# Feed-forward input products of two token blocks formed as seven block products on sums of parts, with features kept in memory

## The chip, the cores and the metric

The kernel runs on 1 core of one Trainium2 chip. The metric is device time in microseconds (us) of one execution; the kernel before took 2666.41 us, the median of 3 runs (2663.89 to 2669.21).

## The reference

The reference is a two-layer encoder in fp32 on 1056 tokens (1024 of a prompt, 32 of a running stream) with 1024 features. Layer 0 mixes by a gated linear recurrence (HGRN2), layer 1 by sliding-window attention. Each mixer is followed by a SwiGLU feed-forward part with 2816 hidden features, and norms stand before and after each part:

```python
x = x + rms_norm(mix, norm_mix_post[layer])
hf = rms_norm(x, norm_ffn_pre[layer])
a, b = jnp.split(hf @ w_ffn_in[layer], 2, axis=-1)
x = x + rms_norm((jax.nn.silu(a) * b) @ w_ffn_out[layer], norm_ffn_post[layer])
```

The change concerns `hf @ w_ffn_in` above all, and the product with `w_ffn_out` behind it.

## The kernel before

**Layout.** Features lie on the 128 partitions, in 8 tiles (`KT`); tokens lie on the free axis in three blocks (`BL`): blocks 0 and 1 of 384 tokens, block 2 of 288. Every fp32 product is three passes of float32r matmuls on a high and a low part of both operands: high x high, high x low, low x high (`mm_fm`, L123 to L133, where L132 is the matmul). Products go to a pool of four PSUM buffers (`mmps`, tile `mm`).

**Weights.** `wunit` (L86 to L103) loads a unit of 128 x 1024 weights (512 KB) into one of two buffers `wst` by a DMA on SP (L90), casts it to `wh` on ACT (L101) and takes the low part `wl` on DVE (L102); `wh` and `wl` have four buffers each. Where a norm's weight is folded in, L97 and L98 do this in pieces.

**Norms.** `postnorm` (L208 to L253) finishes a block behind a mixer or a feed-forward part. It is a generator whose steps are called between other work (`go`, `step`). The sum of squares is taken on PE with a matmul by ones (L180), `newton` (L151 to L160) takes the inverse root on DVE in small operations, `rbcast` (L183 to L190) spreads it over the partitions: a diagonal `dm` on DVE (L185), a matmul by ones (L189) and a copy to `rb` on ACT (L190). Then the rows are scaled (L235), the old x is added (L236, loaded at L218), and `put_x` (L198 to L206) writes the next high and low parts `xh` and `xl`. The x is spilled to memory (L242). Behind a mixer, the scale of the next norm, `rb`, is not put into x: the feed-forward part starts on unscaled x, and `rb` is multiplied in when its products are evicted.

**The feed-forward part** (`ffn`, L256 to L377) has 22 hidden tiles j of 128. For each j and block b, `fin_half` (L264) forms the gate half and the up half, 24 matmuls each (8 feature tiles x 3 passes), from two units of `wfi`. `fin_ev` (L276 to L286) evicts: a multiply by `rb` (L281, L283, DVE), Silu (L282, ACT), a product (L284), and the hidden features' parts `gh` (L285, ACT) and `gl` (L286, DVE), which stay on the chip. `fout` (L320 to L344) forms the output products in parts of `FBLK` = 2, 4, 4, 4, 4, 4 hidden tiles; each part is added into `mix` on DVE (L337; the first copied on ACT, L335). The last part is done block by block, with its weights loaded again for each block, and the `postnorm` of the previous block runs beside it.

**Order.** Every engine takes its instructions in order. A scheduler places the instructions of DVE, ACT, SP and GpSimd (POOL) by priorities that follow the program's order; PE follows the program. The order of the work around the start of the feed-forward part is written by hand in `ffn` (calls of `fin_half` between `go(post1)` and `go(post)`, where `post1` is block 1's mixer norm and `post` block 2's), and in the tables that call steps of block 0's and 1's norms inside the mixers (`fill` in layer 0, `plan` in layer 1).

Of the kernel before, what the change touches and what calls it, by code (L numbers as in the profile page):

```python
# [27 lines left out]
FBLK = [2, 4, 4, 4, 4, 4]  # L28
# [30 lines left out]
def build(nc, tc, I, O):  # L59
# [26 lines left out]
    def wunit(src, scale=None, pieces=1):  # L86
# [16 lines left out]
        return wh, wl  # L103
# [104 lines left out]
    def postnorm(b, mix, acc, w2, xold, wnext, spill, yout, done, more=None):  # L208
# [20 lines left out]
        if yout is None:  # L229
            xs = newx(b)  # L230
            nacc = newacc(b)
        dst = spill if yout is None else yout
        for k in range(KT):
# [4 lines left out]
            if yout is None:  # L238
                put_x(b, k, m, xs, wnext)
                sq_acc(nacc, W, m, k == 0)  # L240
# [4 lines left out]
        if yout is None:  # L245
            done(xs, None, None)
# [9 lines left out]
    def ffn(L, nx, post1, post, wmix, w2, xold, wnext, spill, yout, res):  # L256
# [3 lines left out]
        gpc, gp = pool(f"fg{L}")  # L260
        gs = {}
        wu = {}

        def fin_half(j, b, half):  # L264
            if j not in wu:
                wu[j] = wpair(I[f"wfi{L}"], j)
            if j not in gs:
                gs[j] = (gp.tile([128, NT], F32R, tag="gh", name="gh", bufs=5),
                         gp.tile([128, NT], F32R, tag="gl", name="gl", bufs=5))
# [3 lines left out]
            mm_fm(ps, W, wu[j], 128 * half, lambda k: xh[:, k, :], lambda k: xl[:, k, :])  # L273
            return ps

        def fin_ev(j, b, pa, pb):  # L276
            c0, W = BL[b]
            rb = nx[b][2]
            gh, gl = gs[j]
            ta, tb = tmp(), tmp()  # L280
            nc.vector.tensor_tensor(ta[:, :W], pa[:, :W], rb[:, :W], mult)  # L281
            nc.scalar.activation(ta[:, :W], ta[:, :W], AF.Silu)  # L282
            nc.vector.tensor_tensor(tb[:, :W], pb[:, :W], rb[:, :W], mult)  # L283
            nc.vector.tensor_tensor(tb[:, :W], tb[:, :W], ta[:, :W], mult)  # L284
            nc.scalar.copy(gh[:, c0:c0 + W], tb[:, :W])  # L285
            nc.vector.tensor_tensor(gl[:, c0:c0 + W], tb[:, :W], gh[:, c0:c0 + W].bitcast(F32), sub)  # L286
# [3 lines left out]

        pa = fin_half(0, 0, 0)
# [12 lines left out]
        go(post)  # L304
# [6 lines left out]
        fin_ev(1, 2, pc, fin_half(1, 2, 1))  # L311
        for p in wmix:
            close(p)
        mpc, mp = pool(f"fm{L}", "right")
        mix = mp.tile([128, KT, NT], F32, tag="mix", name="mix")

        last = len(FBLK) - 1
        accs, ts = {}, {}

        def fout(fi, blocks):  # L320
            f = FBLK[fi]
            w = 1024 // f
            base = sum(FBLK[:fi])
            for u in range(f):
                unit = wunit(I[f"wfo{L}"][base + u])
                for m in range(w // 128):
                    k = u * (w // 128) + m
                    for b in blocks:
                        c0, W = BL[b]
                        ps = mmps()  # L330
                        mm_fm(ps, W, [unit], m * 128, lambda q: gs[base + q][0][:, c0:c0 + W],
                              lambda q: gs[base + q][1][:, c0:c0 + W], nk=f, width=w)
                        dst = mix[:, k, c0:c0 + W]
                        if fi == 0:
                            nc.scalar.copy(dst, ps[:, :W])  # L335
                        else:
                            nc.vector.tensor_tensor(dst, dst, ps[:, :W], add)  # L337
                        if fi == last:
                            if k == 0:
                                accs[b] = newacc(b)  # L340
                            sq_acc(accs[b], W, dst, k == 0)
                if fi == last and blocks[0] > 0:
                    for _ in range(steps[blocks[0]][4 + u]):
                        step(blocks[0] - 1)  # L344
# [13 lines left out]
        j = 2  # L358
        for fi in range(1, last):
            for q in range(FBLK[fi]):  # L360
                for b in range(NB):
                    fin(j, b)
                if q == 0:
                    fout(fi - 1, range(NB))
                j += 1


        steps = {1: (1, 2, 1, 1, 1, 0, 1, 1), 2: (1, 2, 1, 1, 1, 0, 0, 1)}
        for b in range(NB):
            for q in range(FBLK[last]):  # L370
                wu.pop(j + q, None)
                fin(j + q, b)
                if b == 0 and q == 0:
                    fout(last - 1, range(NB))
                if b > 0:
                    for _ in range(steps[b][q]):
                        step(b - 1)  # L377
            fout(last, [b])
# [44 lines left out]
    mbs = [mb, mb, None]  # L423
    os = [None] * NB
# [837 lines left out]
```

## Time and profile before

| | |
|---|---|
| median of 3 runs | 2666.41 us (2663.89 to 2669.21) |
| profiled execution | 2668.35 us, of which the span is 2666.6 us |
| granted TensorE clock, mean | 0.986 of full speed |
| DMA traffic | 237.28 MB, mean 89 GB/s |
| feed-forward part of layer 0 | about 670 to 1425 us of the span |
| feed-forward part of layer 1 | about 1870 us to the end |

In the profile, PE is TensorE's matmuls, PEld its weight loads, DVE VectorE, ACT ScalarE, POOL GpSimd and SP the engine that issues the DMAs. L132 is line 132 of the kernel. A group's row ends with the idle time of the engine just before its instructions and with what ended that wait. A waits row has the engine and line, what it waited for, and then total us, times and longest. The execution shown is one; the clock's column PEclk gives the share of full speed that was granted.

### The profile page before, as it was taken

To read this page: it belongs to the slowest core of one execution; us is meant where nothing else is said; L and a number is where in the kernel's file an instruction comes from. 1 tells how busy PE (TensorE), PEld (TensorE's weight loads), DVE (VectorE), ACT (ScalarE), POOL (GpSimd) and SP (SyncE) were. 2 spreads that over 40 slices of the span, in tenths; PEclk is the share of its full clock that TensorE was granted. 3 is DMA by queue.
4 is the path that set the end of the run, shared out by engine and by line. 5 is a ranking of instruction groups with operands and counts; after the bars stand their busy time and mean duration, and the time that the engine had idled before them with its cause. 6 is when DMAs were issued, how large, how long until landed. Compare 5 with 4: busy or idle time off the path is not lost.

```text
span 2666.6 us, 44419 instructions
## 1 busy us (share of the span) xinstructions
PE 2567.9 (96%) x17664; PEld 2466.6 (93%) x17664; DVE 1530.1 (57%) x3464; ACT 975.0 (37%) x2177; POOL 439.8 (16%) x652
## 2 busy tenths in 40 slices
PE   7999998998999999999998999989999999999997
PEld 7899997997999999999998997768999999999997
DVE  8787778778623333334478747786723333333466
ACT  5555555556332121212145324555432121212133
POOL 5442443332100000000024410122200000000012
PEclk9999998999999999999999999989999999999998
DMA  5333333433311111111245642223411111111254
GB/s 163 95 104 95 116 96 116 128 117 123 124 48 43 37 48 48 48 48 53 74 151 166 180 128 74 61 84 100 135 42 39 48 48 48 48 48 48 71 168 147
DMA packets 93336, 237.28 MB, mean 89 GB/s; under 512 B 10008, under 2 KB 46264, under 8 KB 93128
## 3 DMA queue, kind: packets, MB, share of 16 engines
q1 hardware_dynamic: 93128, 234.43, 28.5%
q8 instruction: 139, 2.28, 0.4%
q14 instruction: 69, 0.57, 0.1%
HBM read 210.31 MB, written 24.28 MB: 88 GB/s over the span
## 4 chain that ended last, share of the span: by engine, by line
PE 74%; DVE 14%; ACT 4%; DMA 4%; issue 2%; POOL 1%; SPq 0%; POOLq 0%; DVEq 0%; ACTq 0%
PE mm L132 64%; PE mm L144 4%; DVE wl L102 3%; PE sc L1026 1%; ACT wh L101 1%; PE pav L1084 1%; DMA wst<-in_wfq 1%; DVE wl L98 1%; DVE xl L206 1%; PE ptp L1066 1%; DVE mix L236 1%; DVE at L657 1%; ACT P L1048 1%; DVE mix L235 1%; PE mm L189 1%
## 5 line engine op out<-in xcount | busy, mean ns | idle before, releaser
L132 PE MATMUL mm<-xh,wh 128*128 128x384 f32 (+1 forms) x3120 | 1020.7, 327 | 8.9 <-ACT xh L205 7.5
L132 PE MATMUL mm<-xh,wl 128*128 128x384 f32 (+1 forms) x3120 | 1011.7, 324 | 14.4 <-DVE wl L102 7.8
L132 PE MATMUL mm<-xl,wh 128*128 128x384 f32 (+1 forms) x3120 | 1012.5, 325 | 1.7 <-DVE xl L206 1.5
L132 PEld LDWEIGHTS mm<-xh,wl 128*128 128x128 f32 x3120 | 587.5, 188 | 24.3 <-DVE wl L102 9.8
L132 PEld LDWEIGHTS mm<-xh,wh 128*128 128x128 f32 x3120 | 587.8, 188 | 15.8 <-ACT xh L205 7.5
L132 PEld LDWEIGHTS mm<-xl,wh 128*128 128x128 f32 x3120 | 587.4, 188 | 10.5 <-DVE xl L206 4.0
L102 DVE TENSOR_TENSOR wl<-wst,wh 128x1024 fp32r<-128x1024 f32 (+1 forms) x301 | 374.8, 1248 | 252.0 <-ACT wh L101 251.0
L174 POOL TENSOR_TENSOR acc<-acc,tmp 128x384 f32<-128x384 f32 (+1 forms) x168 | 198.8, 1186 | 1830.4 <-ACT tmp L173 1822.4
L101 ACT CAST wh<-wst 128x1024 fp32r<-128x1024 f32 (+1 forms) x301 | 313.9, 1047 | 470.8 <-PE mm L132 420.6
L132 PE MATMUL mm<-gh,wh 128*128 128x384 f32 (+1 forms) x1056 | 342.3, 325 | 5.8 <-ACT gh L285 4.4
L132 PE MATMUL mm<-gh,wl 128*128 128x384 f32 (+1 forms) x1056 | 341.8, 324 | 4.1 <-DVE wl L102 4.0
L132 PE MATMUL mm<-gl,wh 128*128 128x384 f32 (+1 forms) x1056 | 342.7, 325 | 0.0
L337 DVE TENSOR_TENSOR mix<-mix,mm 128x384 f32<-128x384 f32 (+1 forms) x240 | 124.5, 520 | 235.5 <-PE mm L132 235.3
L283 DVE TENSOR_TENSOR tmp<-mm,rb 128x384 f32<-128x384 f32 (+1 forms) x132 | 68.9, 522 | 240.7 <-PE mm L132 240.6
L132 PEld LDWEIGHTS mm<-gh,wh 128*128 128x128 f32 x1056 | 198.9, 189 | 7.5 <-ACT gh L285 5.9
L132 PEld LDWEIGHTS mm<-gh,wl 128*128 128x128 f32 x1056 | 199.6, 189 | 4.8 <-DVE wl L102 4.8
L132 PEld LDWEIGHTS mm<-gl,wh 128*128 128x128 f32 x1056 | 199.8, 189 | 0.3
L285 ACT CAST gh<-tmp 128x384 fp32r<-128x384 f32 (+1 forms) x132 | 64.2, 486 | 349.7 <-DVE tmp L284 349.7
L144 PE MATMUL mm<-wh,xh 128*128 128x256 f32 (+1 forms) x648 | 185.3, 286 | 2.9 <-ACT vt L510 2.9
L144 PE MATMUL mm<-wh,xl 128*128 128x256 f32 (+1 forms) x648 | 183.1, 283 | 0.0
L144 PE MATMUL mm<-wl,xh 128*128 128x256 f32 (+1 forms) x648 | 182.6, 282 | 0.0
L282 ACT ACTIVATE tmp<-tmp 128x384 f32<-128x384 f32 (+1 forms) x132 | 65.8, 499 | 302.8 <-DVE tmp L281 302.7
(195 smaller groups left out, 2927.0 us busy)
## 6 DMA issues: line engine op xcount, KB each, us to landing
wst<-in_wfi SPq DMA_DIRECT2D x120, 512.0 KB
wst<-in_wfo SPq DMA_DIRECT2D x60, 512.0 KB
wst<-in_wfq SPq DMA_DIRECT2D x47, 512.0 KB
wst<-in_wi SPq DMA_DIRECT2D x24, 512.0 KB
wst<-in_wg SPq DMA_DIRECT2D x24, 512.0 KB
wst<-in_wao SPq DMA_DIRECT2D x24, 512.0 KB
wst<-in_wbo SPq DMA_DIRECT2D x24, 512.0 KB
wst<-in_wq SPq DMA_DIRECT2D x8, 512.0 KB
```

Source lines behind the costliest of these rows:

```text
L98: nc.vector.scalar_tensor_tensor(wl[:, s], st[:, s], pcol(name, k0 + k), wh[:, s].bitcast(F32), mult, sub)
L101: nc.scalar.copy(wh[:, s], st[:, s])
L102: nc.vector.tensor_tensor(wl[:, s], st[:, s], wh[:, s].bitcast(F32), sub)
L132: last_mm[0] = nc.tensor.matmul(ps[:, :W], w, x, start=i == 0, stop=i == n - 1)
L144: last_mm[0] = nc.tensor.matmul(ps[:rows, :256], x, w, start=i == 0, stop=i == n - 1)
L174: nc.gpsimd.tensor_tensor(acc[:, :W], acc[:, :W], q[:, :W], add)
L189: nc.tensor.matmul(ps[:, :W], ones, dm.rearrange("p a b -> p (a b)")[:, :W], start=True, stop=True)
L206: nc.vector.scalar_tensor_tensor(xl[:, k, :], src, pcol(wname, k), xh[:, k, :].bitcast(F32), mult, sub)
L282: nc.scalar.activation(ta[:, :W], ta[:, :W], AF.Silu)
L283: nc.vector.tensor_tensor(tb[:, :W], pb[:, :W], rb[:, :W], mult)
L285: nc.scalar.copy(gh[:, c0:c0 + W], tb[:, :W])
L337: nc.vector.tensor_tensor(dst, dst, ps[:, :W], add)
```

## The change

**Seven products.** For hidden tiles 4 to 21, blocks 0 and 1 are multiplied together as a 2 x 2 matrix product: the rows are two halves of the features (four tiles each), the weights' columns are the gate half and the up half, and the tokens' columns are block 0 and block 1. `fin_7` replaces the eight products of 12 matmuls (four feature tiles x 3 passes) by seven, on sums of weight parts (S1 to S4, `prep`, made for each j on DVE and ACT from the raw unit) and on sums of token parts (T1 to T4, made once per layer), in Winograd's order of sums. Products P1 and P2 accumulate in a PSUM buffer `c11` of its own (two of them); the others are evicted and combined in fp32 tiles `u` on DVE. Block 2 stays as it was, its two halves put between the seven products; for the last two j it comes after the loop. Tiles 0 to 3 stay in the old form for all blocks.

**Normalised x.** Sums of the two blocks need x already scaled. So `postnorm` of blocks 0 and 1 multiplies by `rb` before it writes `xh` and `xl`: for block 1 in place (`full="here"`), for block 0 by reading the spilled x back (`full="back"`). The multiply by `rb` goes from the eviction of these blocks. Two more steps of block 0's norm are called in each mixer's tables.

**Features in memory.** The hidden features are stored to DRAM (`gd`, L309, L454, L459 of the changed kernel) in fp32, and `gload` (L482 to L484) reads them back and splits them. Output products are formed in parts of 2, 8 and 12 (`FBLK` = 2, 8, 4, 8, of which the last two accumulate in the same PSUM buffer), so 64 instead of 160 adds of 384 columns into `mix` and 32 instead of 80 of 288 over both layers. The units of `wfo` are loaded 46 instead of 30 times a layer, those of `wfi` 44 instead of 60 times.

The counts over the whole program: PE's matmuls 16456 to 16024, all of the difference 384 columns wide; DVE instructions 3464 to 3694; ACT 1956 to 2102; DMAs on SP 600 to 814.

The core of the diff:

```diff
-FBLK = [2, 4, 4, 4, 4, 4]
+FBLK = [2, 8, 4, 8]
+NSTD = 4
...
             rbcast(rb, r, W)
+            if full is not None:
+                yield
+                xs = newx(b)
+                for k in range(KT):
+                    if full == "back":
+                        v = tt("xo", 2)[:, :W]
+                        nc.sync.dma_start(v, spill[:, k, :])
+                    else:
+                        v = mix[:, k, :]
+                    nc.vector.scalar_tensor_tensor(v, v, pcol(wnext, k), rb, mult, mult)
+                    put_x(b, k, v, xs, None)
+                    if k == 3:
+                        yield
             done(xs, r, rb)
...
-            nc.scalar.copy(gh[:, c0:c0 + W], tb[:, :W])
-            nc.vector.tensor_tensor(gl[:, c0:c0 + W], tb[:, :W], gh[:, c0:c0 + W].bitcast(F32), sub)
+            nc.sync.dma_start(gd[b][:, j, :], tb)
...
         pa = fin_half(0, 0, 0)
         go(post1)
-        pb = fin_half(0, 0, 1)
-        fin_ev(0, 0, pa, pb)
+        fin_ev(0, 0, pa, fin_half(0, 0, 1))
+        go(post1, 3)
+        pa = fin_half(1, 0, 0)
         go(post)
-        pa = fin_half(0, 1, 0)
-        go(post1)
-        pb = fin_half(0, 1, 1)
-        fin_ev(0, 1, pa, pb)
-        go(post, 2)
-        fin(1, 0)
+        fin_ev(1, 0, pa, fin_half(1, 0, 1))
+        go(post)
+        fin(0, 1)
...
+        def prep(j):
+            un = wu[j] = [wunit(I[f"wfi{L}"][2 * j + k], raw=True) for k in range(2)]
+            (a11, a21), (a12, a22) = [[st.rearrange("p (k c) -> p k c", k=4)[:, :, h * 128:h * 128 + 128]
+                                       for h in range(2)] for (_, _, st) in un]
+            out = []
+            def put(x, y, op):
+                r = sp.tile([128, 4, 128], F32, tag="sr", name="sr", bufs=3)
+                h = sp.tile([128, 4, 128], F32R, tag="sh", name="sh", bufs=7)
+                l = sp.tile([128, 4, 128], F32R, tag="sl", name="sl", bufs=7)
+                nc.vector.tensor_tensor(r, x, y, op)
+                nc.scalar.copy(h, r)
+                nc.vector.tensor_tensor(l, r, h.bitcast(F32), sub)
+                out.append((h, l))
+                return r
+            s1 = put(a21, a22, add)
+            s2 = put(s1, a11, sub)
+            put(a11, a21, sub)
+            put(a12, s2, sub)
+            return out
...
+            mm_7(c11, A(0, 0), B(0, 0))
+            p1 = tmp()
+            nc.scalar.copy(p1, c11[:, :384])
+            p6 = prod(Sk(2), T(2))
+            tt_(u2, p6, p1, add)
+            if with2:
+                pa = fin_half(j, 2, 0)
+            p7 = prod(Sk(3), T(3))
+            tt_(u3, p7, u2, add)
+            p5 = prod(Sk(1), T(1))
+            tt_(u4, p5, u2, add)
+            tt_(u7, p5, u3, add)
+            if with2:
+                fin_ev(j, 2, pa, fin_half(j, 2, 1))
+            mm_7(c11, A(1, 0), B(0, 1), start=False)
+            nc.scalar.activation(ta, c11[:, :384], AF.Silu)
+            p4 = prod(A(1, 1), T(4))
+            tt_(u3, u3, p4, sub)
+            tt_(u3, u3, ta, mult)
+            nc.sync.dma_start(gd[0][:, j, :], u3)
+            p3 = prod(Sk(4), B(1, 1))
+            tt_(u4, u4, p3, add)
+            nc.scalar.activation(u4, u4, AF.Silu)
+            tt_(u7, u7, u4, mult)
+            nc.sync.dma_start(gd[1][:, j, :], u7)
...
+        for b in range(NB):
+            gload(0, b)
+        w0 = [wfo(0, u) for u in range(2)]
+        gload(1, 0)
+        gload(1, 1)
+        for j in range(NF - 2, NF):
+            fin(j, 2)
+        gload(1, 2)
...
-                for h, n in ((0, 1), (1, 2)):
+                for h, n in ((0, 1), (1, 2), (6, 1), (7, 1)):
                     fill[h].append(lambda n=n: go(OP[0], n))
...
-        plan[2] = {u: [(p, 1)] for u in (0, 1, 2, 3, 5, 6)}
+        plan[2] = {u: [(p, 1)] for u in (0, 1, 2, 3, 5, 6, 8, 9)}
```

The scheduled order on DVE in the dense part, from one round of tile j. Before, it holds the evictions of a tile's three blocks (`rb_7698`, `rb_9477` and `rb_9820` are the scales of blocks 0, 1 and 2) and the low parts of the weights:

```order
L281 TENSOR_TENSOR tmp<-mm,rb_7698 128x384
L283 TENSOR_TENSOR tmp<-mm,rb_7698 128x384
L284 TENSOR_TENSOR tmp<-tmp 128x384
L286 TENSOR_TENSOR gl<-tmp,gh 128x384
L281 TENSOR_TENSOR tmp<-mm,rb_9477 128x384
L283 TENSOR_TENSOR tmp<-mm,rb_9477 128x384
L284 TENSOR_TENSOR tmp<-tmp 128x384
L286 TENSOR_TENSOR gl<-tmp,gh 128x384
L281 TENSOR_TENSOR tmp<-mm,rb_9820 128x288
L102 TENSOR_TENSOR wl<-wst,wh 128x1024
```

Now a round begins at the first sum of the next tile's weights (`sr`), and that tile's sums stand between the combinations `u` of this one (`sl` are the sums' low parts):

```order
L387 TENSOR_TENSOR sr<-wst 128x512
L438 TENSOR_TENSOR u<-mm,tmp 128x384
L389 TENSOR_TENSOR sl<-sr,sh 128x512
L387 TENSOR_TENSOR sr<-sr,wst 128x512
L387 TENSOR_TENSOR sr<-wst 128x512
L302 TENSOR_TENSOR tmp<-mm,rb_9848 128x288
L442 TENSOR_TENSOR u<-mm,u 128x384
L389 TENSOR_TENSOR sl<-sr,sh 128x512
L387 TENSOR_TENSOR sr<-wst,sr 128x512
L444 TENSOR_TENSOR u<-mm,u 128x384
L445 TENSOR_TENSOR u<-mm,u 128x384
L389 TENSOR_TENSOR sl<-sr,sh 128x512
```

The rest of the round has a low part `wl`, the eviction of block 2, the last combinations, the second `wl`, and the fourth `sl`.

On DVE at the start of layer 0's feed-forward part, before: the steps of block 2's norm (`r_9433`) run between block 1's `dm` and the evictions.

```order
L102 TENSOR_TENSOR wl<-wst,wh 128x1024
L283 TENSOR_TENSOR tmp<-mm,rb_7698 128x384
L154 TENSOR_SCALAR nv<-mm 128x3
L284 TENSOR_TENSOR tmp<-tmp 128x384
L155 TENSOR_SCALAR r_9433<-nv 128x3
L185 TENSOR_TENSOR dm<-ident,rt_9377 128x384
L156 TENSOR_SCALAR nv<-nv 128x3
```

Now the scaling of block 1's x (`rb_9442` is its scale, L268 the multiply, L204 the low part) stands ahead of them; `r_9515` is block 2's.

```order
L308 TENSOR_TENSOR tmp<-mm,tmp 128x384
L268 SCALAR_TENSOR_TENSOR mixb<-mixb,pv,rb_9442 128x384 x3
L204 TENSOR_TENSOR xl_9449<-mixb,xh_9448 128x384 x3
L268 SCALAR_TENSOR_TENSOR mixb<-mixb,pv,rb_9442 128x384 x3
L204 TENSOR_TENSOR xl_9449<-mixb,xh_9448 128x384 x3
L268 SCALAR_TENSOR_TENSOR mixb<-mixb,pv,rb_9442 128x384 x2
L155 TENSOR_SCALAR nv<-mm 128x3
L204 TENSOR_TENSOR xl_9449<-mixb,xh_9448 128x384
L156 TENSOR_SCALAR r_9515<-nv 128x3
L204 TENSOR_TENSOR xl_9449<-mixb,xh_9448 128x384
```

Block 2's `dm` follows behind the Newton steps, ten rows further down, and PE has the matmul on it ahead of block 1's first product.

On SP at the end of layer 0's hidden tiles, where before loads of weights and of old x stood, the last features of the blocks (`g_0`, `g_1`, `g_2`) are stored and read back (`xl` and `gl` are the buffers that they are read into, `xo` is old x for the norm):

```order
L459 DMA g_1_9348<-u 128x384
L482 DMA xl_13890<-g_1_9348 128x768 x4
L91 DMA wst<-in_wfo 128x1024
L221 DMA xo<-xsa_86 128x384
L91 DMA wst<-in_wfo 128x1024
L221 DMA xo<-xsa_86 128x384 x2
L309 DMA g_2_9349<-tmp 128x288
L482 DMA xl_14018<-g_2_9349 128x576 x2
L309 DMA g_2_9349<-tmp 128x288
L482 DMA xl_14018<-g_2_9349 128x576 x2
L91 DMA wst<-in_wfo 128x1024 x3
```

Each store waits for its feature, and the reads and weights behind it in this queue wait with it.

More of the change, by code (lines that the diff above doesn't have):

```diff
@@ L314, in ffn @@
+        for j in range(NSTD, NF):
+            fin_7(j, j < NF - 2)
+        close(spc)
+        close(tpc)
+        fps.__exit__(None, None, None)
+        gpc, gp = pool(f"fg{L}")
         mpc, mp = pool(f"fm{L}", "right")
         mix = mp.tile([128, KT, NT], F32, tag="mix", name="mix")
-        last = len(FBLK) - 1
-        accs, ts = {}, {}
[L320 to L344, printed above, removed]
@@ new lines, in fmul @@
+        def fmul(ps, fi, b, unit, m, start, stop):
+            f, W = FBLK[fi], BL[b][1]
+            w = 1024 // f
+            gh, gl = G[fi, b]
+            wh, wl = unit
+            for q in range(f):
+                h, l = [t[:, q * w + m * 128:q * w + m * 128 + 128] for t in (wh, wl)]
+                for i, (a, c) in enumerate(((h, gh), (h, gl), (l, gh))):
+                    last_mm[0] = nc.tensor.matmul(ps[:, :W], a, c[:, q, :], start=start and q == i == 0,
+                                                  stop=stop and q == f - 1 and i == 2, skip_group_check=True)
@@ L375, in ffn @@
                 if b > 0:
-                    for _ in range(steps[b][q]):
+                    for _ in range(steps[b][k]):
                         step(b - 1)
-            fout(last, [b])
         close(gpc)
@@ L423, in build @@
     mbs = [mb, mb, None]
+    mbt = [None] * NB
     os = [None] * NB
@@ L430, in outproj @@
         oh, ol = os[b]
-        mix = mbs[b].tile([128, KT, 384], F32, tag="mixb", name="mixb", bufs=1)
+        mix = mbt[b] = mbs[b].tile([128, KT, 384], F32, tag="mixb", name="mixb", bufs=1)
         acc = newacc(b)
@@ L443, in done @@
             nx[b] = r
-        yield from postnorm(b, mix[:, :, :W], acc, w2, xold[b], wnext, spill[b], None, done)
+        yield from postnorm(b, mix[:, :, :W], acc, w2, xold[b], wnext, spill[b], None, done,
+                            full=("back", "here", None)[b])
     def run(g):
```

180 lines of the change are left out of this document (142 added, 38 removed).

## The prediction

> **What bounds the kernel now.** I read the first part of the page, then the chain that ended last.
>
> ```profile
> span 2666.6 us, 44419 instructions
> ...
> PE 2567.9 (96%) x17664; PEld 2466.6 (93%) x17664; DVE 1530.1 (57%) x3464; ACT 975.0 (37%) x2177; POOL 439.8 (16%) x652
> ...
> PE 74%; DVE 14%; ACT 4%; DMA 4%; issue 2%; POOL 1%; SPq 0%; POOLq 0%; DVEq 0%; ACTq 0%
> ```
>
> PE is busy for 2567.9 of 2666.6 us, so it is idle for 98.7 us in all, and three quarters of the last chain is matmuls. The shares are averages over stages, so next come busy times in stretches of 50 us (columns: PE, PEld, DVE, ACT, POOL, granted clock, DMA share, GB/s).
>
> ```profile
> 650.00:700.00 50.00, 42.34 (x252) 39.52 (x251) 38.88 (x82) 22.47 (x46) 13.04 (x13) 1.00 0.45 142
> ...
> 1000.00:1050.00 50.00, 50.00 (x312) 50.00 (x312) 20.74 (x33) 6.11 (x7) 0.00 (x0) 1.00 0.18 53
> 1350.00:1400.00 50.00, 48.13 (x268) 47.54 (x267) 38.17 (x68) 23.80 (x41) 14.07 (x10) 0.97 0.53 159
> ...
> 2000.00:2050.00 50.00, 50.00 (x312) 50.00 (x311) 17.42 (x29) 10.65 (x17) 0.00 (x0) 1.00 0.16 51
> ```
>
> In the middle of both feed-forward parts (near 1000 and 2000 us) PE never pauses, and DVE, ACT and the DMA engines are less than half used. There a matmul less is time less. At the edges (650 and 1350) PE has gaps, and DVE works 38 to 39 of 50 us. So the change spends DVE and DMA where both have room, and whatever it adds at the edges may show.
>
> **The seven products.** The price of a matmul is read from start times on PE in the dense part (start, duration, name).
>
> ```profile
> 901.02 0.29 PE L132 MATMUL mm<-gh,wh 128*128 128x288 f32 x1
> ...
> 902.61 0.35 PE L132 MATMUL mm<-gh,wh 128*128 128x384 f32 x1
> ...
> 906.81 0.29 PE L132 MATMUL mm<-gh,wh 128*128 128x288 f32 x1
> ```
>
> Twelve matmuls of 288 columns lie between the first two rows (1.59 us, 132.5 ns each) and 24 of 384 columns between the second and third (4.20 us, 175 ns each). For each of the 18 hidden tiles 4 to 21 of a layer, blocks 0 and 1 took 2 blocks x 2 halves x 24 = 96 matmuls; seven products of 12 are 84. That is 12 fewer per tile, 36 tiles over both layers, 432 fewer: 432 x 0.1746 = **−75.4 us**. The 288-column matmuls stay, and the output products stay in number.
>
> A page puts another price on it: the Trainium skill, "TensorE: Matmul & The Clock Gate", section "Back-to-back issue gap", gives about 81 ns for 128 columns and 131 ns for 512 in a sustained stream, and N/2.4 + 2.5 ns for an isolated matmul. At 384 columns these make an estimated 114 or 162.5 ns, so 49 or 70 us less in place of 75.4. The trace's 175 ns agrees with neither, and the measurement decides.
>
> **What a tile's round costs DVE.** The 75.4 us come only if the other engines keep pace. From the groups of DVE by shape (total, then mean ns):
>
> ```profile
> L102 DVE TENSOR_TENSOR wl<-wst,wh 128x1024 fp32r<-128x1024 f32 x299 | 373.5, 1251 | 252.0 <-ACT wh L101 251.0
> L337 DVE TENSOR_TENSOR mix<-mix,mm 128x384 f32<-128x384 f32 x160 | 88.4, 553 | 162.7 <-PE mm L132 162.6
> ...
> L286 DVE TENSOR_TENSOR gl<-tmp,gh 128x384 fp32r<-128x384 f32 x88 | 51.0, 580 | 38.9 <-ACT gh L285 38.9
> L284 DVE TENSOR_TENSOR tmp<-tmp 128x384 f32<-128x384 f32 x88 | 50.3, 572 | 7.5
> ...
> L235 DVE SCALAR_TENSOR_TENSOR mixb<-mixb,pv,rb 128x384 f32<-128x384 f32 x32 | 23.2, 747 | 1.6 <-ACT rb L190 1.6
> ...
> L284 DVE TENSOR_TENSOR tmp<-tmp 128x288 f32<-128x288 f32 x44 | 19.9, 452 | 0.0
> ```
>
> The scheduled order has, per tile, two `wl` (2 x 1.25), eight 128x512 operations of the weight sums (between 0.572 at 384 and 1.251 at 1024 columns, so about 0.71 each, an estimate: 5.7), eight of 384 (0.56: 4.5) and three of 288 (0.45: 1.4): 14.0 us. PE's round is 84 x 0.1746 + 48 x 0.1325 = 21.0 us. ACT's groups by shape:
>
> ```profile
> L101 ACT CAST wh<-wst 128x1024 fp32r<-128x1024 f32 x299 | 312.7, 1049 | 469.2 <-PE mm L132 420.6 <-DMA wst<-in_wfo 11.3 <-DMA wst<-in_wfi 10.5
> L282 ACT ACTIVATE tmp<-tmp 128x384 f32<-128x384 f32 x88 | 46.2, 525 | 222.6 <-DVE tmp L281 222.5
> ...
> L190 ACT COPY rb<-mm 128x384 f32<-128x384 f32 x15 | 7.1, 473 | 15.3 <-PE mm L189 15.3
> ```
>
> Two casts of 1.05, four of 512 columns (some 0.62) and four shorter operations of about 0.5 make 6.6 us of ACT. But DVE can't spread its 14.0 us freely. The first sum of the next tile needs both raw units, there are two `wst` buffers, and SP issues the second unit's load behind the store of `g_1`, which waits for the last eviction of the running tile. So a round of DVE is 14.0 us, plus the issue (0.33, in a row below) and the load. Two rows bound the load. In the dense part a `wl` frees a buffer, and a load follows (forty slices of 0.4 us from 1010):
>
> ```profile
> 1013.63 1.23 DVE L102 TENSOR_TENSOR wl<-wst,wh 128x1024 fp32r<-128x1024 f32 x1 [0.49 <-ACT wh L101]
> ```
>
> ```profile
> DMA  0000000000000048897000000000000000000000
> GB/s 0 0 0 0 0 0 0 0 0 0 0 0 0 0 82 195 328 389 297 21 0 0 0 0 0 0 0 0 0 0 0 0 0 0 0 0 0 0 0 0
> ```
>
> The buffer is free at 1014.9 and the engines stop at 1018.0: 3.1 us. In the crowded stretch, by SP's issue and by ACT's first use:
>
> ```profile
> 1390.94 0.33 SPq L90 DMA_DIRECT2D wst<-in_wfo  x1
> ```
>
> ```profile
> 1396.18 1.04 ACT L101 CAST wh<-wst 128x1024 fp32r<-128x1024 f32 x1 [3.23 <-DMA wst<-in_wfo]
> ```
>
> That is 5.2 us. The round is 17.5 to 19.6 us against 21.0, so DVE keeps up with 1.4 to 3.5 us to spare and the cost is 0. I take 4.5 us for the load, since a store of 0.2 MB lies just ahead. The round moves 1.05 MB of weights and 0.54 MB of features, 76 GB/s, half of what the crowded 50 us moved (159). If the cover went, each us would cost 32 us over the rounds of both layers.
>
> **The start of the feed-forward part.** Block 1 is now scaled before its products: eight multiplies and eight low parts on DVE, and they stand ahead of block 2's Newton steps and its `dm`. PE has the broadcast for block 2 ahead of `fin(0, 1)`, and waits for it. Newton's steps and the broadcast, from before:
>
> ```profile
> 677.75 0.16 DVE L155 TENSOR_SCALAR rt<-nv 128x3 int32<-128x3 int32 x1
> ...
> 679.59 0.16 DVE L160 SCALAR_TENSOR_TENSOR rt<-nt,rt 128x3 f32<-128x3 f32 x1
> ...
> 682.00 0.55 DVE L185 TENSOR_TENSOR dm<-ident,rt 128x384 f32<-128x384 f32 x1
> ```
>
> ```profile
> L189 PE MATMUL mm<-dm,ones 128*128 128x384 f32 x30 | 13.3, 524 | 6.4 <-DVE dm L185 6.4
> ```
>
> From PE's broadcast for block 1 on: 0.52, the copy of `rb` on ACT (0.47), 8 x (0.747 + 0.580) = 10.6, Newton 2.3 (677.75 to 679.75, and two rows ahead), one eviction 0.57, `dm` 0.55: 15.0 us. PE has in that time its broadcast and two halves of 4.2: 8.9. It waits **6 us**. Besides, block 1's own Newton had two halves of cover (8.4 us) and now has one. Before, `dm` ended at 682.55, and the feed-forward part had begun here:
>
> ```profile
> 670.36 0.44 PE L132 MATMUL mm<-xh,wh 128*128 128x384 f32 x1 [0.38 <-ACT wh L101]
> ```
>
> That is 12.2 us, where one half and the next (8.4) now cover it: 0 to 3.8, and I take 1.5, because DVE arrives less burdened. Together +7.5 per layer, between 3 and 10.
>
> The burden that goes: block 1's eight low parts in the mixer's last stage (before, in the row below, 0.84 us each), 4.6 to 6.7 us of DVE, where PE waited for DVE (640 to 760 us, total, times, longest; then the same of 1860 to 1960).
>
> ```profile
> L206 DVE SCALAR_TENSOR_TENSOR xl<-mixb,pv,xh 128x384 fp32r<-128x384 f32 x48 | 39.6, 840 | 1.1 <-ACT xh L205 1.1
> ```
>
> ```profile
> PE mm L132 <- DVE wl L98: 6.6, 7, 2.0
> ...
> PE mm L189 <- DVE dm L185: 0.7, 1, 0.7
> ```
>
> ```profile
> PE mm L132 <- DVE wl L102: 6.7, 4, 2.2
> ```
>
> I take −3 per layer, between 0 and −4.6. Block 0's reload and scaling move the other way: about 5 us more DVE in the mixer, in this stretch (70 us; DVE 58.08) and in the attention.
>
> ```profile
> 550.00:620.00 70.00, 69.22 (x686) 64.14 (x685) 58.08 (x226) 39.73 (x121) 24.65 (x58) 1.00 0.35 110
> ```
>
> PE is full there with DVE at 83%, so most of it hides: +2 per layer, between 0 and 5. The sums `T1` to `T4` (40 operations of 0.56, 22 us) lie beside 46 us of tiles 2 and 3 and cost 0.
>
> **From hidden tiles to output products.** Features are read back. Until part 1 starts, parts 0 and 1 (10 x 0.54 MB) and three units (1.6 MB) must land: 7 MB. PE has the last two block-2 tiles (96 x 0.1325 = 12.7) and part 0 (96 x 0.1746 + 48 x 0.1325 = 23.1), 36 us. That needs 195 GB/s; only block 0 is needed at once, so about 160 do, and the fullest row above has 159. On SP the two units of part 0 stand behind the reads of blocks 0 and 1, and block 2's reads behind its last stores, but it is used last. At 150 GB/s it would be 10 us late. I take +3 per layer, between 0 and 10, nearer to the low end because the burst above reached 389 GB/s. The last stage keeps 12 units per block and its PE time, and DVE has less to evict: 0.
>
> **The sum.** Per layer 7.5 − 3 + 2 + 3 = 9.5, twice 19. −75.4 + 19 = −56.4. The profiled execution took 2668.35 us (span 2666.6), 1.94 above the median of the three runs, so 2612.0 there and **2610** as a median.
>
> **Rivals.** *All is covered.* DVE reaches the broadcast early and reads hide: −75.4, so 2591. For it: PE waited only 0.7 us for `dm` at this place before. Against it: the 15.0 us above are mostly rows of DVE in one order.
>
> *The clock drops at the edges.* After a stretch with PE idle over a quarter of the time, the granted clock (third from the right) went to a half:
>
> ```profile
> 1755.00:1760.00 5.00, 3.75 (x33) 2.41 (x32) 5.00 (x11) 2.97 (x12) 1.94 (x2) 1.00 0.15 57
> 1760.00:1765.00 5.00, 3.44 (x19) 2.27 (x16) 5.00 (x11) 2.87 (x11) 2.00 (x1) 0.72 0.14 43
> 1765.00:1770.00 5.00, 4.80 (x26) 2.50 (x24) 3.92 (x10) 2.69 (x9) 3.08 (x2) 0.50 0.46 155
> 1770.00:1775.00 5.00, 3.84 (x20) 2.83 (x20) 3.51 (x10) 3.04 (x12) 1.02 (x1) 0.50 0.36 118
> 1775.00:1780.00 5.00, 4.67 (x21) 4.27 (x19) 2.34 (x5) 1.49 (x3) 0.56 (x2) 0.50 0.00 0
> 1780.00:1785.00 5.00, 5.00 (x26) 2.90 (x24) 3.54 (x19) 3.27 (x11) 0.00 (x0) 0.73 0.01 3
> ```
>
> The lost clock adds up to 5 x (0.28 + 0.5 + 0.5 + 0.5 + 0.27) = 10 us. One drop at each layer's 6 us wait gives +20: 2630; with the reads at their upper end as well (+14), 2644. I call this case 2640. Against it: the waits of up to 2.0 us in the mixer's last stage left the clock at 1.00 (row of 650). The Trainium skill, "TensorE: Matmul & The Clock Gate", "Part 1: The HAM clock gate", says that an idle PE is set back to half rate and that it needs about 3.4 us of work to get out; by it a drop would cost an estimated 1.7 us, 3.4 in all, and the sum would be −53. The rows show some 20 us below full rate, so they set this rival's price.
>
> *Slower: the weights' loads bind.* Stores and loads share SP's order, and the second load is always the last. The round is 14.4 us plus the load; it passes 21.0 at a load of 6.7 us, takes all of the gain (56.4 / 32 = 1.8) at 8.4, and makes the kernel slower beyond. At 10 us: 32 x 3.3 − 56.4 = +50, so 2716. For it: loads and stores collide at the same moment of each round. Against it: the longest load in the crowded rows took 5.2.
>
> *It does nothing:* PE's matmuls are the dense part's only limit, so no change needs costs that happen to match the gain.
>
> **Chances.** The forecast 0.48 (its own range 2597 to 2624), all covered 0.20, clock drops or late reads 0.26, slower 0.05, no change 0.01. A measurement of this kernel tells about 0.2% (5 us) from no change; faster by more than that is 0.94, within it 0.01, slower 0.05. The low end is the covered case with the mixer's relief in part, 2588; the high end takes in most of the clock case, 2645.
>
> **What would show it.** Right: matmuls 175 ns apart through the rounds, rounds of 21.0 us, DVE some 14 us busy in each with a wait for `wst` before the first `sr`; one PE wait near 6 us for `dm` at each start. Wrong: PE waiting for `sl`, `wl` or an eviction inside the rounds (load over 6.7 us), rounds longer than 21.0, a granted clock under 1.00 after the starts, or PE waiting for `wst` or feature reads at the first output products.

## The result and the profile after

The changed kernel took 2574.45 us (median of 4 runs, 2569.65 to 2579.3) against 2666.64 us of the kernel before on the same occasions: a ratio of 0.9654, interval 0.9634 to 0.9675. It is 92 us faster. The forecast was 2610 us, and 2574 lies below the range's low end of 2588. The direction was right; the gain came out at 92 us where 56 were forecast.

The first part of the page of the changed kernel and its last chain:

```profile
span 2573.6 us, 44368 instructions
...
PE 2484.7 (97%) x17232; PEld 2388.2 (93%) x17232; DVE 1695.1 (66%) x3694; ACT 1074.3 (42%) x2323; POOL 453.9 (18%) x652
...
PE 77%; DVE 12%; ACT 4%; DMA 3%; issue 2%; POOL 2%; SPq 0%; POOLq 0%; ACTq 0%; DVEq 0%
```

PE's busy time fell by 83.2 us (2567.9 to 2484.7), 7.8 more than the 75.4 of the removed matmuls, and its idle time by 9.8 (98.7 to 88.9). DVE works 165 us more. Busy times of the same four stretches of 50 us as before (PE, PEld, DVE, ACT, POOL, granted clock, DMA share, GB/s):

```profile
650.00:700.00 50.00, 46.19 (x244) 44.44 (x245) 33.77 (x79) 20.11 (x39) 10.56 (x11) 0.90 0.46 146
1000.00:1050.00 50.00, 50.00 (x318) 50.00 (x317) 30.95 (x51) 15.80 (x24) 0.00 (x0) 1.00 0.21 65
1350.00:1400.00 50.00, 44.56 (x300) 43.04 (x299) 37.08 (x69) 21.57 (x38) 21.56 (x15) 0.97 0.54 172
2000.00:2050.00 50.00, 50.00 (x313) 50.00 (x312) 29.78 (x49) 16.15 (x26) 0.00 (x0) 1.00 0.30 94
```

In the dense parts PE is full as before and DVE went from 17 to 21 us of 50 to 30 to 31.

Where did the 93.0 us of the span go? The norms' broadcasts (matmuls on `dm`) stand at the same places of the program in both kernels, so their start times cut the span into pieces. All pieces but those of the feed-forward products have the same matmuls in both kernels, with one exception: the broadcast at 1787.9 us stands behind 16 score matmuls (`sc`) that follow it in the changed kernel, so the attention and its end are one piece here. The two broadcasts that bound the largest difference outside the feed-forward products, of the kernel before, and of the changed one (start, duration):

```profile
420.54 0.81 PE L189 MATMUL mm<-dm,ones 128*128 128x384 f32 x2
...
556.56 0.91 PE L189 MATMUL mm<-dm,ones 128*128 128x384 f32 x2
```

```profile
418.75 0.81 PE L190 MATMUL mm<-dm,ones 128*128 128x384 f32 x2
...
544.02 0.91 PE L190 MATMUL mm<-dm,ones 128*128 128x384 f32 x2
```

| piece, in the kernel before | before | after | difference |
|---|---|---|---|
| begin to 420.5 | 420.5 | 418.8 | −1.8 |
| 420.5 to 556.6, layer 0's mixer | 136.0 | 125.3 | −10.8 |
| 556.6 to 641.6, its end | 85.0 | 88.8 | +3.8 |
| 641.6 to 718.8, start of feed-forward | 77.2 | 78.0 | +0.8 |
| 718.8 to 1516.4, feed-forward and norms | 797.7 | 755.8 | −41.9 |
| 1516.4 to 1849.9, attention and its end | 333.5 | 330.6 | −2.9 |
| 1849.9 to 1921.4, start of feed-forward | 71.5 | 71.9 | +0.4 |
| 1921.4 to the end, feed-forward | 745.2 | 704.5 | −40.6 |

The differences are those of the unrounded times. The feed-forward pieces hold the 37.7 us of each layer's matmuls and a few more. The rest lies in the mixers, where the change removes no matmul at all: −10.8 in layer 0's mixer and +3.8 behind it, and −2.9 in the attention.

### The profile page after: what moved, and what is told of

It reads as the page before. It is cut to its first block, busy times and chain, and to the rows that moved or that the text cites. A ratio compares the mean times of both kernels' runs of the same rounds, so it can differ in the third digit from the quotient of the medians.

```text
span 2573.6 us, 44368 instructions
## 1 busy us (share of the span) xinstructions
PE 2484.7 (97%) x17232; PEld 2388.2 (93%) x17232; DVE 1695.1 (66%) x3694; ACT 1074.3 (42%) x2323; POOL 453.9 (18%) x652
## 4 chain that ended last, share of the span: by engine, by line
PE 77%; DVE 12%; ACT 4%; DMA 3%; issue 2%; POOL 2%; SPq 0%; POOLq 0%; ACTq 0%; DVEq 0%
PE mm L133 28%; PE mm L495 17%; PE mm L404 15%; PE c L404 6%; PE mm L145 5%; DVE wl L103 2%; PE sc L1218 1%; PE pav L1276 1%; ACT wh L102 1%; PE ptp L1258 1%; DVE wl L99 1%; PE mm L190 1%; DVE mixb L240 1%; DMA xl<-g 1%; DVE mixb L239 1%
## 5 line engine op out<-in xcount | busy, mean ns | idle before, releaser
L133 PE MATMUL mm<-xh,wh 128*128 128x384 f32 (+1 forms) x1968 | 634.4, 323 | 8.1 <-ACT xh L206 7.1
L133 PE MATMUL mm<-xh,wl 128*128 128x384 f32 (+1 forms) x1968 | 626.5, 318 | 12.2 <-DVE wl L103 8.4
L133 PE MATMUL mm<-xl,wh 128*128 128x384 f32 (+1 forms) x1968 | 628.6, 319 | 1.0 <-DVE xl L207 0.8
L133 PEld LDWEIGHTS mm<-xh,wl 128*128 128x128 f32 x1968 | 373.4, 190 | 20.0 <-DVE wl L103 9.3
L133 PEld LDWEIGHTS mm<-xh,wh 128*128 128x128 f32 x1968 | 374.1, 190 | 15.2 <-ACT xh L206 7.1
L133 PEld LDWEIGHTS mm<-xl,wh 128*128 128x128 f32 x1968 | 373.9, 190 | 9.9 <-issue 3.9
L495 PE MATMUL mm<-xh,wl 128*128 128x384 f32 (+1 forms) x768 | 247.5, 322 | 1.7 <-DVE wl L103 1.7
L495 PE MATMUL mm<-xl,wh 128*128 128x384 f32 (+1 forms) x768 | 247.5, 322 | 0.0
L495 PE MATMUL mm<-xh,wh 128*128 128x384 f32 (+1 forms) x768 | 247.1, 322 | 0.0
L388 ACT CAST sh<-sr 128x512 fp32r<-128x512 f32 x144 | 89.5, 622 | 175.6 <-PE mm L404 147.9
L495 PEld LDWEIGHTS mm<-xh,wl 128*128 128x128 f32 x768 | 144.2, 188 | 2.1 <-DVE wl L103 2.1
L495 PEld LDWEIGHTS mm<-xh,wh 128*128 128x128 f32 x768 | 144.1, 188 | 0.0
L495 PEld LDWEIGHTS mm<-xl,wh 128*128 128x128 f32 x768 | 144.1, 188 | 0.0
L145 PEld LDWEIGHTS mm<-wh,xh 128*128 128x128 f32 (+1 forms) x648 | 119.0, 184 | 3.5 <-ACT vt L702 2.1
L145 PEld LDWEIGHTS mm<-wh,xl 128*128 128x128 f32 (+1 forms) x648 | 119.0, 184 | 0.8
L145 PEld LDWEIGHTS mm<-wl,xh 128*128 128x128 f32 (+1 forms) x648 | 118.5, 183 | 0.5
```

The costliest lines, as they stand in the source:

```text
L133: last_mm[0] = nc.tensor.matmul(ps[:, :W], w, x, start=i == 0, stop=i == n - 1)
L145: last_mm[0] = nc.tensor.matmul(ps[:rows, :256], x, w, start=i == 0, stop=i == n - 1)
L388: nc.scalar.copy(h, r)
L495: last_mm[0] = nc.tensor.matmul(ps[:, :W], a, c[:, q, :], start=start and q == i == 0, stop=stop and q == f - 1 and i == 2, skip_group_che ...
```

## The experiments

Theory: the seven products are worth their matmuls. The mixers gained because block 0's early high and low parts (`put_x`, sixteen operations on ACT and DVE) left a stretch in which DVE is full and PE waits for it; the work that stands later in their place costs less there. Rivals: the seven products are worth more than their matmuls; or clock drops fall by chance and the place of `put_x` does not matter.

**Eight products, the rest kept.**

```diff
-            fin_7(j, j < NF - 2)
+            for b in range(NB if j < NF - 2 else 2):
+                fin(j, b)
```

The calls of `t123` and `t4` go too.

> All hidden tiles in the old form with eight products (no sums of weights or tokens); normalised x, features in memory and the new output parts are kept. Theory: the seven products are worth their 432 matmuls at 175 ns and nothing else, so this kernel is 75.4 us above the changed one, 2650 us (ratio to before 0.994), and the other 17 us of the gain stay. Rival: the other edits are worth nothing or cost the 19 us that the prediction gave them, and the seven products brought 92 to 111 us; then 2667 to 2686 us.

Measured: 2656.1 us, ratio 0.9954 (0.994 to 0.9968). The changed kernel is 0.0300 ± 0.0025 below it, 80 ± 7 us. So the seven products are worth their 75.4 us within the measurement, and 12 us of gain stand without them. In the profile the two pieces of feed-forward are 36.0 and 42.0 us longer than in the changed kernel.

**Block 0's early parts put back.** The first pass of `postnorm` writes them as before the change, and the late ones overwrite them:

```diff
-            if full is None:
+            if full != "here":
                 xs = newx(b)
...
-                if full is None:
+                if full != "here":
                     put_x(b, k, m, xs, wnext)
```

> The changed kernel, with block 0's first high and low parts also written where they were before the change (they are overwritten later, so it is work without use). Theory: the extra gain came from taking these sixteen operations out of a stretch of each mixer in which DVE was full and PE waited for it, with a drop of the granted clock behind; so 11 us come back in layer 0 and 5 us in layer 1: 2591 us (ratio 0.972), with the clock at 0.5 to 0.8 after about 445 us. Rival: the clock drops fall by chance and the place of these operations does not matter: 2575 us (0.965).

Measured: 2587.38 us, ratio 0.9695 (0.9682 to 0.9708), 0.0041 ± 0.0024 above the changed kernel: 11 ± 6 us come back. In the profile 8.4 us of it lie in the mixer's piece of layer 0, which lasts 133.7 us again (420.96 to 554.64). The attention with its end lasts 335.4 us (333.5 before, 330.6 in the changed kernel), but it varies as much between profiles that have no early parts (see the last experiment). Busy times of the stretch in layer 0, of the kernel before, of the changed kernel, and of this one:

```profile
440.00:450.00 10.00, 6.14 (x40) 4.97 (x38) 10.00 (x31) 5.42 (x14) 4.55 (x4) 0.90 0.33 117
450.00:460.00 10.00, 6.49 (x39) 4.90 (x38) 8.21 (x22) 2.21 (x6) 0.25 (x2) 0.50 0.10 19
460.00:470.00 10.00, 10.00 (x93) 9.22 (x93) 7.59 (x23) 4.06 (x8) 4.16 (x8) 0.91 0.52 161
```

```profile
440.00:450.00 10.00, 5.12 (x25) 4.81 (x24) 8.65 (x27) 3.06 (x8) 2.13 (x3) 0.66 0.41 133
450.00:460.00 10.00, 10.00 (x115) 9.31 (x113) 9.09 (x28) 6.79 (x16) 1.18 (x4) 1.00 0.36 107
```

```profile
440.00:450.00 10.00, 5.74 (x40) 4.39 (x38) 10.00 (x30) 5.51 (x15) 4.64 (x4) 1.00 0.31 104
450.00:460.00 10.00, 6.20 (x44) 5.19 (x44) 9.43 (x28) 2.08 (x6) 0.25 (x2) 0.66 0.21 58
```

With `put_x` there, DVE is full for 10 us and PE is busy for about 6 of 10 twice in a row; without it, PE is full from 450 on. In the kernel before, three of the low parts stand on DVE between the operations that PE waits for:

```profile
442.80 0.60 DVE L206 SCALAR_TENSOR_TENSOR xl<-mixb,pv,xh 128x384 fp32r<-128x384 f32 x1
...
450.03 0.60 DVE L206 SCALAR_TENSOR_TENSOR xl<-mixb,pv,xh 128x384 fp32r<-128x384 f32 x1
...
452.94 0.61 DVE L206 SCALAR_TENSOR_TENSOR xl<-mixb,pv,xh 128x384 fp32r<-128x384 f32 x1
```

PE's waits between 420 and 560 us, of the kernel before (total, times, longest):

```profile
PE pgt L789 <- DVE xl L792: 3.2, 3, 2.0
PE psA L676 <- DVE XX L586: 2.5, 1, 2.5
PE pu L729 <- ACT kT L725: 1.6, 1, 1.6
PE po L772 <- DVE Sq L746: 1.4, 1, 1.4
PE pgt L789 <- DVE ro L160: 0.9, 1, 0.9
PE mm L132 <- DVE wl L102: 0.5, 1, 0.5
PE pgt L789 <- DVE at L648: 0.2, 1, 0.2
```

And of the changed kernel, all of them over 0.1 us:

```profile
PE mm L133 <- DVE wl L103: 4.9, 1, 4.9
PE po L964 <- DVE Sq L938: 0.4, 1, 0.4
```

Nine small waits, seven of them between 441 and 458 us, became one of 4.9 and one of 0.4. Busy times of the whole piece tell what falls on the waits and what on the clock (the kernel before, its repetition below, this kernel, the changed one):

```profile
420.54:556.56 136.02, 125.53 (x1061) 117.72 (x1060) 104.05 (x324) 77.37 (x194) 48.97 (x102) 0.94 0.41 125
```

```profile
418.36:553.87 135.51, 124.80 (x1061) 117.38 (x1060) 104.68 (x324) 77.33 (x195) 48.83 (x102) 0.94 0.39 126
```

```profile
420.96:554.64 133.68, 122.74 (x1061) 115.71 (x1059) 104.81 (x324) 77.18 (x194) 48.62 (x102) 0.96 0.40 127
```

```profile
418.75:544.02 125.27, 119.81 (x1062) 114.60 (x1060) 100.94 (x316) 72.33 (x186) 48.33 (x102) 0.97 0.44 136
```

PE is idle for 10.5, 10.7, 10.9 and 5.5 us (length less PE's busy time). The traces' clock records have 17.1, 17.1, 10.2 and 6.8 us at 0.50 in the piece, of which half is lost: 8.5, 8.5, 5.1 and 3.4 us. So of the 10.8 us that the changed kernel gains here, about 5 are waits and 5 are clock. Putting the early parts back returned all of the waits, and 1.7 us of the clock.

**Block 0 alone normalised late.** The kernel before, with `full="back"` for block 0 only (the lines of the change's `postnorm`, tables, and no multiply by `rb` for this block).

> The kernel before, with only block 0's x normalised late (read back from memory, scaled, split) instead of early; the feed-forward parts are otherwise as before. Theory: 16 us gained where the early parts stood, 6.5 us lost where the late ones stand: 2657 us (ratio 0.996). Rival (moving them only adds work, as the prediction had it): 4 to 7 us more than before, 2672 us (1.002).

Measured: 2661.8 us, ratio 0.9975 (0.9964 to 0.9986): faster by 7 us with no other part of the change, a little less than the 10 expected, and not slower, as the rival had it. Its piece from 420.82 to 546.34 lasts 125.5 us, and the one behind it 88.0 (85.0 before). The attention with its end lasts 335.6 us, no less than before (333.5).

**Blocks 0 and 1 normalised before the feed-forward part.** As the last, with `full="here"` for block 1 and the changed kernel's order of the first products.

> The kernel before, with blocks 0 and 1 both normalised before the feed-forward part and its first products ordered as in the changed kernel; features, products and output parts are as before. Theory: as with block 0 alone, the start costs about 1 us net per layer: 2658 us (0.997). Rival (the prediction's terms for the start): 9 us more, 2667 us (1.000). What lies between this kernel and the one with eight products is the work of features in memory and larger output parts: some 7 us by the theory.

Measured: 2663.06 us, ratio 0.9986 (0.9977 to 0.9996). Between the expectations of the two theories, and not to be told from the kernel with block 0 alone. The kernel with eight products is 0.0032 ± 0.0017 below it, 9 ± 5 us: features in memory and larger output parts gained something too, where the prediction had a cost of 6. DVE has less to evict and add at the end of each layer, but little of the gain is seen in PE's waits. Those at the end of layer 0, of the kernel before (1412 to 1517 us) and of the changed one (1362 to 1467):

```profile
PE mm L189 <- DVE dm L185: 6.4, 4, 3.1
PE mm L132 <- DVE wl L102: 4.0, 2, 2.1
PE mm L132 <- DVE mix L337: 1.3, 1, 1.3
PE mm L132 <- ACT gh L285: 0.7, 1, 0.7
```

```profile
PE mm L190 <- DVE dm L186: 7.0, 4, 4.7
PE mm L495 <- DVE wl L103: 3.2, 3, 1.5
```

That is 12.4 against 10.2 us. Where more of it comes from is taken up under the output products below.

**The weight units of the seven-product tiles loaded twice.**

```diff
-            nc.sync.dma_start(st[:, s], src[:, s])
+            for _ in range(2 if raw else 1):
+                nc.sync.dma_start(st[:, s], src[:, s])
```

> The changed kernel, with both raw weight units of tiles 4 to 21 loaded twice into the same buffer, one load behind the other (the second brings the same data). In each round of the changed kernel DVE waits about 2 us for the last load, and later 2.7 us for PE, which is what the load can grow before PE waits. Theory (the prediction's rival of loads that bind, with this spare time): a second load adds some 3 to 4 us to a round's wait, of which 2.7 are covered, so 0.3 to 1.3 us in 32 rounds: 10 to 42 us more than the changed kernel, 2585 to 2616 us (ratio 0.969 to 0.981). Rival: other slack in the round absorbs the load, 2575 us (0.965).

Measured: 2577.87 us, ratio 0.9666 (0.9653 to 0.968): not to be told from the changed kernel, and the theory's 10 us or more did not come. DVE's groups between 800 and 1060 us, of the changed kernel, then of this one (last: idle just before them):

```profile
L387 DVE TENSOR_TENSOR sr<-wst 128x512 f32<-128x512 f32 x25 | 17.2, 689 | 25.8 <-DMA wst<-in_wfi 25.8
...
L452 DVE TENSOR_TENSOR u<-u,mm 128x384 f32<-128x384 f32 x13 | 7.2, 554 | 35.6 <-PE mm L404 35.6
```

```profile
L388 DVE TENSOR_TENSOR sr<-wst 128x512 f32<-128x512 f32 x24 | 16.5, 688 | 60.4 <-DMA wst<-in_wfi 60.4
...
L453 DVE TENSOR_TENSOR u<-u,mm 128x384 f32<-128x384 f32 x13 | 7.2, 551 | 12.0 <-PE mm L405 11.9
```

The wait for the weights grew from 2.1 to 5.0 us a round (25.8 and 60.4 over some 12 rounds), the wait for PE fell from 2.7 to 0.9 (35.6 and 12.0 over 13). The order of DVE differs a little too. In layer 0's rounds PE did not pause:

```profile
800.00:1100.00 300.00, 300.00 (x1887) 300.00 (x1886) 180.40 (x304) 90.18 (x144) 0.00 (x0) 1.00 0.41 129
```

In layer 1 one round lasted 22.6 us in place of 21.0, with a PE wait of 1.3 us for DVE in it. So the spare time of the round is real, and was nearly used up; the second transfer cost less than the 3 to 4 us that were expected.

**Block 2's broadcast later on PE.**

```diff
-        go(post)
-        fin(0, 1)
+        pa = fin_half(0, 1, 0)
+        go(post)
+        fin_ev(0, 1, pa, fin_half(0, 1, 1))
```

> The changed kernel, with block 2's broadcast half a product later on PE (behind the first half of hidden tile 0 of block 1), so that DVE has 4.2 us more before it is waited for. Theory: the wait of 2.84 us for dm at each layer's start goes, and with it the drop of the clock in layer 0, while block 2's x comes some 1.5 us later than its first use: 2 to 4 us less in all, 2571 us (ratio 0.964), at the edge of what can be measured. Rival: block 2's x becomes the next wait, and nothing or 3 us are lost: 2575 to 2578 us.

Measured: 2567.53 us, ratio 0.9632 (0.9618 to 0.9645), 7 us below the changed kernel's median, but with intervals that overlap; hence the repetition below. The wait for `dm` went (660 to 700 us, of the changed kernel, then of this one):

```profile
PE mm L190 <- DVE dm L186: 2.8, 1, 2.8
```

```profile
PE mm L133 <- DVE wl L103: 0.4, 1, 0.4
```

No wait for block 2's x took its place.

**Seven products from hidden tile 3 on.**

```diff
-NSTD = 4
+NSTD = 3
...
-        fin(3, 1)
-        fin(3, 0)
-        fin(3, 2)
```

> The changed kernel with the seven products from hidden tile 3 on (before: from 4 on). Theory: 24 matmuls of 384 columns fewer (4.2 us), but the sums of tokens T1 to T4 (22 us of DVE) then stand beside 23 us of PE work and not 46, so some of it comes back as a wait before the first rounds: 2570 to 2580 us (ratio 0.964 to 0.967). Rival: the sums had no need of the cover, 2570 us; or they need all of it, and 2 x 15 us are lost: 2600 us (0.975).

Measured: 2576.56 us, ratio 0.9663 (0.965 to 0.9676), no difference. Its waits at the first round (730 to 750 us; the same in layer 1):

```profile
PE mm L401 <- ACT sh L385: 1.6, 1, 1.6
PE c L401 <- ACT tmp L432: 1.0, 1, 1.0
```

That is 5.2 us over both layers, and takes back the 4.2 that the matmuls save. The cover of 46 us for the token sums is needed in part.

**Three repetitions on one chip.**

> The changed kernel once more, unedited, beside the next two on one chip: 2574 us (ratio 0.965). Theory: the clock drop after the wait at the start of layer 0's feed-forward part and the shorter drop after 440 us come back in its profile, since the same waits precede them. Rival: the drops lie elsewhere, and the gain in the mixer's stretch was chance.

Measured: 2573.37 us, ratio 0.9652 (0.9637 to 0.9668). Its piece of the mixer lasted 125.4 us (419.09 to 544.45), and the clock was at 0.50 between 445 and 450 us, as the theory had it. But the drop at the start of feed-forward, which the first profile has, is missing in this one. 675 to 690 us, of the first profile and of this:

```profile
675.00:680.00 5.00, 2.16 (x11) 1.87 (x10) 3.93 (x17) 0.86 (x2) 0.00 (x0) 0.88 0.11 39
680.00:685.00 5.00, 5.00 (x16) 4.71 (x16) 3.70 (x9) 1.69 (x4) 0.00 (x0) 0.50 0.26 75
685.00:690.00 5.00, 5.00 (x28) 5.00 (x28) 3.00 (x8) 1.34 (x3) 0.00 (x0) 0.94 0.49 161
```

```profile
675.00:680.00 5.00, 2.33 (x14) 2.01 (x12) 4.48 (x18) 1.03 (x2) 0.00 (x0) 1.00 0.11 39
680.00:685.00 5.00, 4.83 (x27) 4.75 (x28) 3.66 (x10) 1.70 (x4) 0.00 (x0) 1.00 0.24 72
```

> The kernel with block 2's broadcast half a product later, once more, beside the changed kernel on the same chip. Theory: 4 to 7 us less than the changed kernel (two waits of 2.84 us and what the clock loses after the first). Rival: no difference that can be measured.

Measured: 2566.91 us, ratio 0.9623 (0.9607 to 0.964), 0.0029 ± 0.0023 below the changed kernel beside it, 8 ± 6 us; the medians differ by 6.5. It is the fastest version here. Two waits of 2.84 us, one per layer, make 5.7.

> The kernel before once more, unedited, for a second profile. Theory: DVE is full and PE waits between 440 and 460 us again, with the clock at 0.5 behind it, and the stretch from the broadcast at 420 us to the next one lasts 136 us as in the first profile. Rival: the clock drop was chance, and the stretch lasts 125 us as in the changed kernel.

Measured: 2665.86 us in one run. The stretch of 420 to 560 us repeats: 418.36 to 553.87, 135.5 us, with the clock at 0.50 between 450 and 455. Over all profiles the piece lasted 136.0, 135.5 and 133.7 us where the early parts stand there and 125.0 to 125.8 us in the nine where they do not. That it is their place, and not chance, is shown for layer 0. For the attention it is not shown: with its end it lasted 333.5, 332.4 and 335.4 us with them, and 330.6 to 335.6 without.

## Why the prediction was wrong, point by point

The forecast was a saving of 75.4 us less 19 us of costs at the edges. The saving came; in place of the costs, the mixers, the starts and what else the feed-forward pieces hold brought some 16 us more.

**The seven products: right.** −75.4 was the term; the rounds from one first product to the next last 21.0 us, as worked out (the first matmul of `c` in two rounds that follow each other):

```profile
761.58 0.34 PE L404 MATMUL c<-xh,wh 128*128 128x384 f32 x1
...
782.58 0.34 PE L404 MATMUL c<-xh,wh 128*128 128x384 f32 x1
```

All 32 full rounds last 21.0 us, and the kernel with eight products is 80 ± 7 us slower. The Trainium skill's "TensorE: Matmul & The Clock Gate", "Back-to-back issue gap", would have given an estimated 49 or 70 us, and was rightly left aside.

**DVE keeps up: right, with a slip.** The operation of 512 columns took 0.69 us (0.71 estimated). DVE has 2.1 + 2.7 us to spare per round, of which the second is what a longer load can take. But the last load stands behind the store of `g_0`, not `g_1`: the rows of SP show the load at 845.96 and the store of `g_1` at 847.58.

**The move of block 0's normalisation: this is the step that failed.** The prediction took block 0's reload and scaling as "about 5 us more DVE in the mixer" and +2 per layer, +4 in all. It priced the place where the work arrived and not the place that it left. In layer 0 the early parts left a stretch where DVE was full and PE waited for it: −10.8 us, half of it waits and half clock, against +3.8 where the late ones stand. Alone, with no other part of the change, the move was worth −7 ± 3 us (the third experiment). The stretch after 1755 us stood in the prediction, as the price of a clock drop in a rival; that the change takes DVE's work out of that very stretch was not asked. What this saved in the attention is not shown: −2.9 us in the profiles of the table, within what that piece varies by.

**The start of feed-forward: mis-sized.** +7.5 − 3 per layer was the term; the pieces show +0.8 and +0.4. Block 1's Newton caused no wait, and block 2's `dm` one of 2.84 us per layer in place of 6. The 0.7 us wait for `dm` that the prediction put at this place stood behind it, at a later broadcast (718.8 us), and is still there. The eight multiplies and low parts took 8.3 us (668.19 to 676.5) and not 10.6: the multiply took 0.615 us in place of the 0.747 of a like row, and Newton's rows ran between them. The relief of −3 was seen (the waits for `wl` L98 of 6.6 us became 2.1 for the same line, L99, in layer 0).

**The output products: wrong sign.** +3 per layer was the term. Nothing was late: PE waited 0.9 us at most at a time, and the reads came in at more than the 195 GB/s that were needed (1125 to 1165 us of the changed kernel):

```profile
DMA packets 3575, 8.57 MB, mean 214 GB/s; under 512 B 402, under 2 KB 1298, under 8 KB 3571
```

In its place the feed-forward pieces gained 7.1 us beyond the removed matmuls, and features in memory with the larger parts are worth 9 ± 5 us by the fourth experiment. PE's idle time in these pieces hardly changed (32.1 us before, 31.5 after, both layers), and no more did the lost clock (11.9 and 12.2 us). What did change is the spacing of matmuls that follow one another within 0.2 us: 174.9 ns at 384 columns and 132.4 at 288 before, 174.0 and 132.2 in the changed kernel, which over some 5650 and 3010 of them is 5.9 us. The kernel with eight products lies between, at 174.4 and 132.3. So the term's mechanism, late reads, did not occur; why the spacing shrank the runs do not show.

**The sum again.** −75.4 for the products, −10.8 + 3.8 in layer 0's mixer and its end, −2.9 in the attention, +1.2 at the starts, −7.1 for the rest of the feed-forward pieces and −1.8 at the beginning make −93.0. The last is as large as what two profiles of one kernel differ by there (420.5 and 418.4), and explains nothing.

**Rivals.** "All is covered" at 2591 was nearest, but it also has no place for a gain. The clock's drop behind the wait for `dm` came in one of the changed kernel's two profiles, in layer 0 alone, and the clock that it lost adds up to 5 x (0.12 + 0.50 + 0.06) = 3.4 us, not 10. After the wait that ended at 679.5 us the clock was back some 6 us later, not some 20 as in the prediction's rows. The Trainium skill's "TensorE: Matmul & The Clock Gate", "Part 1: The HAM clock gate", has the clock come back after some 3.4 us of work, and the 6 us are nearer to that. The prediction's 20 us belong to a stretch where PE kept pausing.

## What to carry to other kernels

When work moves, look up both places: where one engine is full and the bound engine waits for it, taking work out can gain time although the work as a whole grows. Repeated short waits can cost as much again in clock (5 us of each in layer 0's mixer). Before a difference between two pieces of the span is read, check that they hold the same instructions, and compare several profiles of each kernel: the attention up to 1787.9 us is 5.5 us shorter in the changed kernel, but it holds 16 matmuls fewer there. Price the saved matmuls from their spacing and check the other engines by a full round (their work plus the one transfer that stands in order), since this part of the sum came out within the measurement. When a wait for a small chain remains, moving the waiting matmul behind half a product is worth trying: it gave 6.5 us by the medians here.

## What the runs showed of the hardware

In all twelve profiles, every drop of the granted clock that begins and ends inside the span goes to 0.50 and lasts a whole multiple of 3.4 us (3.4 to 20.5), by the traces' clock records. The same wait of 2.84 us for the same instruction at the start of layer 0 came with such a drop (3.4 or 6.8 us, begun just before the wait's end) in three of the six profiles that have the wait and with none in the other three, so a single wait of this length does not decide the drop. A DVE multiply of 384 columns by a column and `rb` took 0.60 to 0.82 us in the mean, by the line of the changed kernel that it stood in. Doubling the weights' loads in the dense rounds, to 129 GB/s, cost nothing that could be measured.
